# Second MLP: eight pairs plain on the first token pair instead of ten, the forming steps closer together

## The chip, the cores and the metric

The kernel runs on one core of one Trainium2 chip. The metric is the device time of one execution in microseconds (us). The kernel before took 2447.15 us, the median of three runs (2445.96, 2447.15, 2447.61).

Engines are named as in the profile: PE is the matmul engine (PEld its weight loads), DVE the vector engine, ACT the scalar engine, POOL the general engine, SP the engine whose queue issues the DMAs here.

## The reference

The reference is one step of a two-layer encoder over 1024 prompt tokens and 32 sample tokens, 1056 in all. What matters here is the second layer's MLP, the last large piece of work:

```python
u = x * (1 + sc2) + sh2
f = jnp.square(jax.nn.relu(u @ p['w_up'][l])) @ p['w_down'][l]
x = layer_norm(ALPHA * x + (1 + g2) * f, p['ln_g'][l, 1], p['ln_b'][l, 1])
```

D_MODEL is 1024 and D_FF is 4096. All data are float32.

## The kernel before

**Splits.** A float32 operand is held as two parts, high and low: ACT casts the high part (L89) and DVE subtracts it to get the low part (L90). Each product of a 128x128 block is then three matmuls (high by high, high by low, low by high), without the low by low.

**The second MLP** is `mlp7`, called once, with the settings of class `L1`. The 1056 tokens are four quarters of 264 (`QN`); two quarters are a token pair `tp`. Token pair 1 (quarters 3 and 2) comes first, token pair 0 second. The 4096 hidden columns are 16 pairs `pb` of 2x128 columns. For each hidden pair and token pair the up projection gives a 2x2 set of results, and it has two ways to do it:

- *Plain* (`up_tile`): for each of 2 column halves and 2 quarters, 24 matmuls of 264 columns (L118, L119, L120), 96 in all. It needs two split weight blocks of the pair (`w_up`, each loaded by a DMA of 512 KB into `raw_up` and split by one ACT and one DVE instruction of 128x1024).
- *Seven products* (class `Seven`, L1300): Winograd's form of the 2x2 product, with seven products of 12 matmuls, 84 in all. It needs formed weights (`forms`: sums and differences of the four weight blocks, four DVE subtractions of 128x512 and seven splits of 128x512, for each hidden pair once) and formed tokens (`tforms`, for each token pair once: in the sequence t3, ext, t1, TF, TF, u, 14 instructions of 128x1056 on DVE and 4 casts on ACT).

Either way four results are gathered in a tile `H`. When they are there, `h_forms` squares them, forms sums and differences for the down projection, splits them into `HL` and `HM` (one buffer each) and writes them to DRAM (`hd`, or `hpl` for pairs 14 and 15).

**The order.** Token pair 1 is ready before token pair 0, since the normalization (`norm`) that gives the tokens goes block by block. So a list `FIRST` of hidden pairs is done plainly on token pair 1 while the rest is made ready. Three of them come in the loop over `L.ready`; the others are `rest`. A counter `at` numbers the halves of `rest` so that the last has 13; a table says which forming steps are put in behind which half: step 0 is one step of `tforms` for token pair 1, step 1 one for token pair 0, step 2 one of `forms` for the first weights. After each pair of `rest`, the plain weights of the pair after next are asked for. Then the list `seq` gives the jobs of seven products: a pair in `FIRST` has the one job that is left (token pair 0), any other has two. Two jobs overlap on PE: the products are sorted by 7j+2i, for job j and product i. The variable `lone` is the last job on token pair 1; behind it the rooms of its tokens are given over to the loads `fx` of the down projection (`fill`, at products 2, 4, 6 from two jobs after `lone`), 14 tiles of 528 KB for its first group.

**What sets the order on the engines.** A scheduler places the instructions of DVE, ACT, SP and, in the plain part, PE by its own reckoning, from the order in the code; in the seven products PE's order is the code's (`manual_schedule`). Each engine then works through its own list strictly in order. The raw tiles of loaded weights, the tiles t3 and t1 of `tforms` and the loads `rdn_u` of `forms` share three buffers (`raw`); split weights share six (`wc`).

Of the kernel before, what the change touches and what calls it, by code (L numbers as in the profile page):

```python
# [75 lines left out]
def trunk_kernel(ctx: ExitStack, tc: tile.TileContext, a, o):  # L76
# [88 lines left out]
    def ada_part(l, i):  # L165
        return ada[:, l * 48 + i * KC:l * 48 + (i + 1) * KC, :]
# [954 lines left out]
    def up_weights(l, pb):  # L1121
        return [wblock(f"up{l}_{pb}_{i}", a["w_up"][l], 512 * i, pb * 256) for i in range(2)]

    def mlp7(L):
# [17 lines left out]
        def up_w(pb):  # L1142
            if pb not in wups:
                wups[pb] = up_weights(l, pb)
            return wups[pb]
# [33 lines left out]
        def up_tile(pb, f, q):  # L1179

            tp = q // 2
            ps = up_mm(pb, f, q)
            if (pb, tp) not in hts:
                hts[pb, tp] = [h_tile(pb, tp), 0]
            H = hts[pb, tp][0]
            nc.scalar.activation(H[:, ((1, 0), (3, 2))[f][q % 2]], ps, AF.Relu)
            hts[pb, tp][1] += 1
            if hts[pb, tp][1] == 4:
                h_forms(pb, tp, hts.pop((pb, tp))[0])
            flow.tick(QN / 96)  # L1190
# [9 lines left out]
        def tforms(tp, ext):  # L1200

            def b(i):
                kap, q = {B11: (0, 0), B12: (0, 1), B21: (1, 0), B22: (1, 1)}[i]
                return [L.u4(hl, tp, kap, q) for hl in range(2)]

            def raw(i):
                return raw_tile([P, 4, QN], f"t{i}_{l}_{tp}")

            def less(t, x, y):
                nc.vector.tensor_sub(t, x[0].bitcast(F32), y)  # L1210
                nc.vector.tensor_add(t, t, x[1].bitcast(F32))

            def diff(t, x, y):
                less(t, x, y[0].bitcast(F32))
                nc.vector.tensor_sub(t, t, y[1].bitcast(F32))
            t3 = raw(3)
            diff(t3, b(B22), b(B12))
            yield
            split(ext[:, 0], ext[:, 1], t3)
            yield  # L1220
            t1 = raw(1)
            diff(t1, b(B12), b(B11))
            yield
            split(TF[tp, 0][0], TF[tp, 0][1], t1)
            less(t1, b(B22), t1)
            yield
            split(TF[tp, 1][0], TF[tp, 1][1], t1)
            less(t1, b(B21), t1)
            yield
            split(*b(B12), t1)  # L1230
# [95 lines left out]
        seq = L.seq  # L1326
# [4 lines left out]
        def prep(n):  # L1331
            if n < len(makers):
                preps[n] = makers[n]()
                next(preps[n])
# [21 lines left out]
        for j, pb in enumerate(rest):  # L1356
            for f in range(2):
                for q in L.quarters[:2]:
                    up_tile(pb, f, q)
                if (j, f) == (0, 1):  # L1360
                    L.ready(2)
                    for n, tp in enumerate(L.pairs):
                        for i, t in enumerate(L.scratch(n)):
                            TF[tp, i] = t
                    exts[tp1] = ring.tile([P, 2, KG, QN], F32R, tag="wc", name=f"exu_{l}", bufs=6)
                    tfs = [tf, tforms(tp1, exts[tp1])]
                at = 2 * j + f - 2 * len(rest) + 14
                if at == 11:
                    prep(0)
                for n in {2: (1,), 3: (1,), 4: (1,), 5: (1,), 6: (1,), 7: (1,), 8: (0,), 9: (0,), 11: (0, 2),  # L1370
                          12: (2,), 13: (2, 0)}.get(at, ()):
                    if n < 2:
                        next(tfs[n], None)
                    else:
                        got[0] = next(preps[0])
            del wups[pb]
            if j + 2 < len(rest):
                up_w(rest[j + 2])
# [48 lines left out]
        with tc.manual_schedule(engines={mybir.EngineType.PE}):  # L1427
            for _, j, i in sorted((7 * j + 2 * i, j, i) for j in range(len(jobs)) for i in range(7)):
                n, tp = jobs[j]
# [439 lines left out]
    for ti in rev:  # L1869
        t0, n = TBS[ti]  # L1870
# [33 lines left out]
        for k in range(KC):  # L1904
            gain_shift(ti, 1, k)
    wup1 = {}
    FIRST = [6, 7, 8, 9, 10, 11, 12, 13, 14, 15]

    def early_up(ti, pr):

        if ti == rev[-1] and pr:
            wup1[FIRST[pr - 1]] = up_weights(1, FIRST[pr - 1])
    out_proj([(0,), (1, 2, 3)], rev, wo_get, o_mov, ada_part(1, 2), end_out1, "b", width=[384, 384, 320],
             after_pr=early_up)

    class L1:
# [2 lines left out]
        order, blocks = rev, [(0, 288), (288, 256), (544, 256), (800, 256)]  # L1919
        pairs, quarters = (1, 0), (3, 2, 1, 0)  # L1920
        first = FIRST
        seq = [(pb, (0,) if pb in FIRST else (1, 0)) for pb in (0, 6, 1, 7, 2, 8, 3, 9, 4, 10, 5, 11, 14, 12, 15, 13)]

        def u(hl, k, q):
            return u2[q // 2][:, hl, k, q % 2 * QN:(q % 2 + 1) * QN]
# [40 lines left out]
        def after(blk):  # L1966
            t0, n = blk
            tiles = [(t, min(P, t0 + n - t)) for t in range(t0, t0 + n, P)]
            flow.add(norm_out(tiles, L1.put_out, L1.next_y, L1.gb, blk == L1.blocks[-1]), TAIL[0])
    mlp7(L1)  # L1970
    flow.finish()
    psD_cm.__exit__(None, None, None)
# [36 lines left out]
```

## Time and profile before

| | |
|---|---|
| median of three runs | 2447.15 us |
| the profiled execution, its own time | 2451.64 us |
| its span, first to last instruction | 2449.7 us |
| mean granted clock of PE | 0.993 |
| busy share of the span: PE, DVE, ACT, POOL | 97%, 78%, 45%, 7% |
| DMA over the span | 137 GB/s |

The profiled execution is 4.49 us longer than the median of the runs; of that, 1.94 us lie outside its span. In the span, the plain part of the second MLP runs from about 1731 us, its seven products from 1854 to 2083 us, the down projection from there to the end. The busy share of PE counts pipelined matmuls as busy from start to end, so the share of a stretch says only whether it stood still at all; how long a matmul takes of PE's time is seen in the distance from one start to the next.

### The profile page before, as it was taken

How to read it: one execution, taken by the hardware profiler on the slowest of the kernel's cores; microseconds unless marked ns; L12 is line 12 of the kernel's file. 1: busy time of each engine (PE TensorE's matmuls, PEld its weight loads, DVE VectorE, ACT ScalarE, POOL GpSimd, SP SyncE). 2: the span in 40 equal slices, each digit the busy share in tenths (PEclk: the TensorE clock that was granted, in tenths of full speed). 3: DMA queues.
4: the chain of work that ended last, by engine and by line, in shares of the span. 5: the costliest groups of instructions: out<-in, count | busy, mean ns of one | idle time of the engine just before them, and what ended most of it. 6: DMA issues, size and time to landing. Idle time of an engine off the chain costs nothing.

```text
span 2449.7 us, 42910 instructions
## 1 busy us (share of the span) xinstructions
PE 2386.9 (97%) x16580; PEld 2294.7 (94%) x16580; DVE 1919.8 (78%) x4340; ACT 1090.7 (45%) x2264; POOL 167.3 (7%) x315
## 2 busy tenths in 40 slices
PE   7999999999999999999999999999999999899997
PEld 4999999999999999999999977789999999899997
DVE  4899998788678678687488666755998888887878
ACT  4554456283212212212157466763776777222212
POOL 0211100000000000000000224420000000000003
PEclk9999999999999999999999999999999999999999
DMA  7432223412233233233223230041486779966642
GB/s 287 137 102 88 89 80 109 157 35 87 89 101 121 87 104 113 82 116 107 89 77 101 64 73 2 10 117 42 159 275 233 255 256 335 376 234 230 228 156 72
DMA packets 251503, 335.15 MB, mean 137 GB/s; under 512 B 12824, under 2 KB 201644, under 8 KB 250276
## 3 DMA queue, kind: packets, MB, share of 16 engines
q1 hardware_dynamic: 251300, 332.42, 41.4%
q8 instruction: 130, 2.13, 0.4%
q14 instruction: 73, 0.60, 0.1%
HBM read 255.50 MB, written 79.24 MB: 137 GB/s over the span
## 4 chain that ended last, share of the span: by engine, by line
PE 76%; DVE 12%; DMA 4%; ACT 3%; issue 2%; POOL 0%; SPq 0%; ACTq 0%; DVEq 0%; POOLq 0%
PE dn L1409 11%; PE up L1300 6%; PE up L118 6%; PE up L120 6%; PE up L119 6%; PE dn L119 5%; PE dn L118 5%; PE dn L120 5%; PE pv L1749 3%; PE s L1692 2%; PE pt L1727 2%; PE o L118 1%; PE o L119 1%; PE o L120 1%; DMA hd<-HL 1%
## 5 line engine op out<-in xcount | busy, mean ns | idle before, releaser
L1409 PE MATMUL dn<-fx,wf_d 128*128 128x264 f32 x2016 | 254.2, 285 | 6.9 <-DVE ACX L986 3.3
L1409 PEld LDWEIGHTS dn<-fx,wf_d 128*128 128x128 f32 x2016 | 248.7, 188 | 9.3 <-issue 2.9
L119 PE MATMUL dn<-h,w_dn 128*128 128x384 f32 (+1 forms) x768 | 249.5, 325 | 0.0
L118 PE MATMUL up<-U,w_up 128*128 128x384 f32 (+1 forms) x768 | 249.2, 324 | 0.0
L119 PE MATMUL up<-U,w_up 128*128 128x384 f32 (+1 forms) x768 | 247.9, 323 | 0.0
L118 PE MATMUL dn<-h,w_dn 128*128 128x384 f32 (+1 forms) x768 | 247.8, 323 | 0.0
L120 PE MATMUL up<-U,w_up 128*128 128x384 f32 (+1 forms) x768 | 247.6, 322 | 0.0
L120 PE MATMUL dn<-h,w_dn 128*128 128x384 f32 (+1 forms) x768 | 247.3, 322 | 0.0
L986 DVE SCALAR_TENSOR_TENSOR ACX<-dn,ada,ACX 128x264 f32<-128x264 f32 (+5 forms) x400 | 160.1, 426 | 52.6 <-PE dn L1409 39.6
L238 DVE SCALAR_TENSOR_TENSOR aacc<-rada,cs,aacc 128x256 f32<-128x256 f32 x448 | 190.1, 476 | 0.0
L986 DVE SCALAR_TENSOR_TENSOR acc<-dn,ada,acc 128x384 f32<-128x384 f32 (+2 forms) x256 | 119.2, 485 | 47.0 <-PE dn L120 45.6
L1025 ACT ACTIVATE r<-up 128x384 f32<-128x384 f32 (+1 forms) x96 | 44.3, 463 | 243.3 <-PE up L120 236.9
L119 PEld LDWEIGHTS dn<-h,w_dn 128*128 128x128 f32 x768 | 144.5, 188 | 0.2 <-DVE h L1028 0.2
L120 PEld LDWEIGHTS dn<-h,w_dn 128*128 128x128 f32 x768 | 144.5, 188 | 0.0
L120 PEld LDWEIGHTS up<-U,w_up 128*128 128x128 f32 x768 | 144.3, 188 | 0.0
L118 PEld LDWEIGHTS up<-U,w_up 128*128 128x128 f32 x768 | 144.2, 188 | 0.1
L119 PEld LDWEIGHTS up<-U,w_up 128*128 128x128 f32 x768 | 144.2, 188 | 0.0
L118 PEld LDWEIGHTS dn<-h,w_dn 128*128 128x128 f32 x768 | 143.9, 187 | 0.2
L1300 PE MATMUL up<-u,wf_u 128*128 128x264 f32 x1056 | 139.6, 284 | 1.3 <-ACT wf_u L89 0.6
L1300 PEld LDWEIGHTS up<-u,wf_u 128*128 128x128 f32 x1056 | 132.6, 188 | 1.9 <-ACT wf_u L89 0.8
L1027 DVE TENSOR_TENSOR r<-r 128x384 f32<-128x384 f32 (+1 forms) x96 | 49.9, 522 | 103.3 <-ACT h L1026 102.9
L89 ACT CAST w_up<-raw_up 128x1024 fp32r<-128x1024 f32 x52 | 54.3, 1046 | 136.4 <-DMA raw_up<-in_w_up_dram 102.5
(386 smaller groups left out, 6575.0 us busy)
## 6 DMA issues: line engine op xcount, KB each, us to landing
rada<-in_w_ada_dram SPq DMA_DIRECT2D x64, 512.0 KB
hd<-HL SPq DMA_DIRECT2D x28, 1056.0 KB
raw_up<-in_w_up_dram SPq DMA_DIRECT2D x52, 512.0 KB
fx<-hd SPq DMA_DIRECT2D x50, 528.0 KB
hd<-HM SPq DMA_DIRECT2D x28, 792.0 KB
raw_dn<-in_w_down_dram SPq DMA_DIRECT2D x36, 512.0 KB
ada_room<-in_w_ada_dram SPq DMA_DIRECT2D x32, 512.0 KB
rdn_u<-in_w_up_dram SPq DMA_DIRECT2D x32, 512.0 KB
```

The source lines that it names most:

```text
L89: nc.scalar.copy(dst_h, src)
L118: nc.tensor.matmul(ps, wh, mov(0, k), start=(k == 0), stop=False)
L119: nc.tensor.matmul(ps, wh, mov(1, k), start=False, stop=False)
L120: nc.tensor.matmul(ps, wl, mov(0, k), start=False, stop=(k == nk - 1))
L238: nc.vector.scalar_tensor_tensor(acc[:, cnd], raw[:, k], sc, acc[:, cnd], op0=ALU.mult, op1=ALU.add)
L986: nc.vector.scalar_tensor_tensor(xs, ps[:, off + o:off + o + mm_], gate[:, fc, cnd:cnd + 1], xs, op0=ALU.mult, op1=ALU.add)
L1027: nc.vector.tensor_mul(r, r, r)
L1300: nc.tensor.matmul(p, self.ws[w][:, wl, k], moving(f, tp, xl, k), start=first and k + n_ == 0, stop=k == 3 and n_ == 2, skip_group_check=n ...
L1409: nc.tensor.matmul(p, ws[w][:, wl, k], t[:, s0, xl], start=first and k + n_ == 0, stop=k == kg - 1 and n_ == 2, skip_group_check=not first)
L1692: nc.tensor.matmul(s[:, b, :w], qst, kk[i][:, g, k0 + j0:k0 + j0 + w], start=(i == 0), stop=(i == 1))
L1727: nc.tensor.transpose(pt[:kp, j - j0, pr * P:(pr + 1) * P], ps_[pr][:, j * P:j * P + kp], ident)
L1749: nc.tensor.matmul(pv[64 * e:64 * e + 64, :nq], V[:kp, vt0 + j, g * 64:(g + 1) * 64], pts[e][:kp, j, :nq], start=(j == 0), stop=(j == nt - 1))
```

## The change

Two hidden pairs, 6 and 7, leave `FIRST`. On token pair 1 they are done by seven products instead of plainly, so there are 24 jobs of seven products instead of 22, and `rest` is five pairs instead of seven. The order of `seq` is made anew for that: three times two pairs with two jobs stand side by side, and the jobs behind `lone` are five instead of six. The counter `at` now runs from 4 to 13, and `tforms` for token pair 0 has its steps at 5, 6, 7, 8, 8, 9 instead of 2 to 7; the steps for token pair 1 are at 9, 10, 11, 13 instead of 8, 9, 11, 13. The steps for the first weights stay where they were, counted from the end.

```diff
-                for n in {2: (1,), 3: (1,), 4: (1,), 5: (1,), 6: (1,), 7: (1,), 8: (0,), 9: (0,), 11: (0, 2),
+                for n in {5: (1,), 6: (1,), 7: (1,), 8: (1, 1), 9: (1, 0), 10: (0,), 11: (0, 2),
                           12: (2,), 13: (2, 0)}.get(at, ()):
...
-    FIRST = [6, 7, 8, 9, 10, 11, 12, 13, 14, 15]
+    FIRST = [8, 9, 10, 11, 12, 13, 14, 15]
...
-        seq = [(pb, (0,) if pb in FIRST else (1, 0)) for pb in (0, 6, 1, 7, 2, 8, 3, 9, 4, 10, 5, 11, 14, 12, 15, 13)]
+        seq = [(pb, (0,) if pb in FIRST else (1, 0)) for pb in (0, 8, 1, 9, 2, 3, 10, 4, 5, 11, 6, 7, 14, 12, 15, 13)]
```

The first place is DVE's list from the point where the tokens of pair 0 are complete. `H1_9_1` is the tile of hidden pair 9 on token pair 1, `t3_1_0` and `t1_1_0` are the forming tiles of token pair 0, `w_up1_12_0` the first plain weight block of pair 12. Before:

```order
L1170 TENSOR_TENSOR H1_9_1_18851<-H1_9_1_18851 128x528
L1210 TENSOR_TENSOR t3_1_0_19046<-u2_0_18049 128x1056
L1211 TENSOR_TENSOR t3_1_0_19046<-t3_1_0_19046,u2_0_18049 128x1056
L90 TENSOR_TENSOR HL1_9_1_18961<-H1_9_1_18851,HL1_9_1_18961 128x4x264
L1215 TENSOR_TENSOR t3_1_0_19046<-t3_1_0_19046,u2_0_18049 128x1056
L1173 TENSOR_TENSOR H1_9_1_18851<-H1_9_1_18851 128x264
L1170 TENSOR_TENSOR H1_10_1_19018<-H1_10_1_19018 128x528
L1174 TENSOR_TENSOR H1_9_1_18851<-H1_9_1_18851 128x264
L90 TENSOR_TENSOR exu_1_18982<-t3_1_0_19046,exu_1_18982 128x1056
L90 TENSOR_TENSOR w_up1_12_0_19118<-raw_up1_12_0_19116,w_up1_12_0_19118 128x1024
```

And now:

```order
L1210 TENSOR_TENSOR t3_1_0_18983<-u2_0_18049 128x1056
L90 TENSOR_TENSOR HL1_11_1_18961<-H1_11_1_18851,HL1_11_1_18961 128x4x264
L1211 TENSOR_TENSOR t3_1_0_18983<-t3_1_0_18983,u2_0_18049 128x1056
L1173 TENSOR_TENSOR H1_11_1_18851<-H1_11_1_18851 128x264
L1215 TENSOR_TENSOR t3_1_0_18983<-t3_1_0_18983,u2_0_18049 128x1056
L1174 TENSOR_TENSOR H1_11_1_18851<-H1_11_1_18851 128x264
L90 TENSOR_TENSOR w_up1_13_0_18989<-raw_up1_13_0_18987,w_up1_13_0_18989 128x1024
L90 TENSOR_TENSOR HM1_11_1_18968<-H1_11_1_18851,HM1_11_1_18968 128x3x264
L1170 TENSOR_TENSOR H1_12_1_19022<-H1_12_1_19022 128x528
L1210 TENSOR_TENSOR t1_1_0_19116<-u2_0_18049 128x1056
```

At the same point of the norm, the first weights to be split behind it are those of the sixth pair of `FIRST` now (pair 13), and were those of the seventh (pair 12).

The second place is SP's list, from the DMA that writes the normalized tokens to DRAM (`xsp2`), at the same point of the norm. Before:

```order
L1865 DMA xsp2_79<-ACC0_17431 128x4x384
L96 DMA raw_up1_12_0_19116<-in_w_up_dram 128x4x256
L1865 DMA xsp2_79<-ACC1_17432 128x4x384
L1172 DMA hd1_3_1_18345<-HL1_9_1_18961 128x4x528
L96 DMA raw_up1_12_1_19121<-in_w_up_dram 128x4x256
```

And now:

```order
L1865 DMA xsp2_79<-ACC0_17431 128x4x384
L96 DMA raw_up1_13_0_18987<-in_w_up_dram 128x4x256
L1865 DMA xsp2_79<-ACC1_17432 128x4x384
L1172 DMA hd1_4_1_18347<-HL1_11_1_18961 128x4x528
L96 DMA raw_up1_13_1_18992<-in_w_up_dram 128x4x256
```

The loads of pair 13 stand where those of pair 12 stood: the writes of the tokens and of an `HL` are ahead of them.

The third place is DVE's list at the last plain weights, those of pair 15, and the first formed weights (`wf_u1_0_0`, of hidden pair 0). Before:

```order
L90 TENSOR_TENSOR w_up1_15_0_19521<-raw_up1_15_0_19519,w_up1_15_0_19521 128x1024
L90 TENSOR_TENSOR HL1_13_1_19504<-H1_13_1_19419,HL1_13_1_19504 128x4x264
L90 TENSOR_TENSOR TF0_18980<-t1_1_1_19447,TF0_18980 128x1056
L1173 TENSOR_TENSOR H1_13_1_19419<-H1_13_1_19419 128x264
L1210 TENSOR_TENSOR t1_1_1_19447<-u2_1_17466,t1_1_1_19447 128x1056
L1174 TENSOR_TENSOR H1_13_1_19419<-H1_13_1_19419 128x264
L1211 TENSOR_TENSOR t1_1_1_19447<-t1_1_1_19447,u2_1_17466 128x1056
L90 TENSOR_TENSOR HM1_13_1_19511<-H1_13_1_19419,HM1_13_1_19511 128x3x264
L90 TENSOR_TENSOR w_up1_15_1_19526<-raw_up1_15_1_19524,w_up1_15_1_19526 128x1024
L90 TENSOR_TENSOR TF0_18980<-t1_1_1_19447,TF0_18980 128x1056
L90 TENSOR_TENSOR wf_u1_0_0_19650<-rdn_u1_0_0_19642,wf_u1_0_0_19650 128x512
```

And now:

```order
L90 TENSOR_TENSOR u2_0_18049<-t1_1_0_19116,u2_0_18049 128x4x264
L90 TENSOR_TENSOR HM1_13_1_19251<-H1_13_1_19155,HM1_13_1_19251 128x3x264
L1211 TENSOR_TENSOR t1_1_1_19257<-t1_1_1_19257,u2_1_17466 128x1056
L1215 TENSOR_TENSOR t1_1_1_19257<-t1_1_1_19257,u2_1_17466 128x1056
L90 TENSOR_TENSOR w_up1_15_0_19263<-raw_up1_15_0_19261,w_up1_15_0_19263 128x1024
L90 TENSOR_TENSOR w_up1_15_1_19268<-raw_up1_15_1_19266,w_up1_15_1_19268 128x1024
L90 TENSOR_TENSOR TF0_18980<-t1_1_1_19257,TF0_18980 128x1056
L90 TENSOR_TENSOR HL1_14_1_19381<-H1_14_1_19296,HL1_14_1_19381 128x4x264
L1210 TENSOR_TENSOR t1_1_1_19257<-u2_1_17466,t1_1_1_19257 128x1056
L90 TENSOR_TENSOR wf_u1_0_0_19396<-rdn_u1_0_0_19388,wf_u1_0_0_19396 128x512
```

The weights of pair 15 stand ahead of both TF splits of token pair 1 now (one of the two stood ahead of the second block before), and all forming of token pair 0 stands ahead of them, as before.

## The prediction

> **What bounds the kernel now.** I read the page first, then what PE waited for in the plain part, then busy time by stretch, and then the order of time on DVE, SP and ACT from 1790 to 1876 us. The page's first rows:
>
> ```profile
> span 2449.7 us, 42910 instructions
> PE 2386.9 (97%) x16580; PEld 2294.7 (94%) x16580; DVE 1919.8 (78%) x4340; ACT 1090.7 (45%) x2264; POOL 167.3 (7%) x315
> ```
>
> PE bounds the kernel as a whole, but the change touches two short stages in which something else is as full. The stretches (the columns are length, then PE, PEld, DVE, ACT, POOL busy, granted clock, DMA share, GB/s):
>
> ```profile
> 1780.00:1800.00 20.00, 20.00 (x166) 20.00 (x166) 19.85 (x32) 17.07 (x28) 0.00 (x0) 1.00 0.74 257
> 1800.00:1820.00 20.00, 17.29 (x139) 16.87 (x139) 19.16 (x22) 13.38 (x19) 0.00 (x0) 1.00 0.94 311
> 1820.00:1840.00 20.00, 20.00 (x166) 19.95 (x165) 20.00 (x22) 13.86 (x20) 0.00 (x0) 1.00 0.78 261
> 1900.00:1950.00 50.00, 50.00 (x413) 50.00 (x412) 43.32 (x75) 36.62 (x63) 0.00 (x0) 1.00 0.69 240
> 2080.00:2100.00 20.00, 17.13 (x128) 15.69 (x127) 18.22 (x43) 8.26 (x15) 0.00 (x0) 1.00 1.02 359
> 2100.00:2120.00 20.00, 17.69 (x139) 16.93 (x139) 17.70 (x51) 5.39 (x14) 0.00 (x0) 1.00 1.02 386
> ```
>
> From 1780 to 1840 DVE is busy 59 of 60 us: the plain part has no DVE time left. In the seven products (1900 to 1950) PE never stands and DVE is 87% busy. At the start of the down projection (2080 on) the DMA engines are full and PE stands some 2.5 us in 20. What PE waited for from 1740 to 1860:
>
> ```profile
> PE up L118 <- ACT w_up L89: 2.0, 1, 2.0
> PE up L120 <- DVE w_up L90: 0.9, 2, 0.7
> ```
>
> So already now PE's only waits in the plain part are for split weights.
>
> **What the change saves on PE.** The rows: a product's 12 matmuls, and where the fourth plain pair starts.
>
> ```profile
> 1768.45 0.29 PE L118 MATMUL up<-u,w_up 128*128 128x264 f32 x1
> 1900.96 1.61 PE L1300 MATMUL up<-u,wf_u 128*128 128x264 f32 x12
> 1902.41 1.62 PE L1300 MATMUL up<-exu,wf_u 128*128 128x264 f32 x12
> 1854.18 2.01 PE L1300 MATMUL up<-u,wf_u 128*128 128x264 f32 x15
> ```
>
> Twelve matmuls take 1.46 us from start to start, 0.122 each. A plain pair is 96 x 0.122 = 11.7 us, a job of seven products 84 x 0.122 = 10.2. Two pairs moved save 24 matmuls, 2.9 us, if PE is the bound. The plain part loses 23.4 us of PE work, the seven products gain 20.5.
>
> **What it does to DVE in the plain part.** DVE's rows give the prices, from one start to the next:
>
> ```profile
> 1792.89 1.02 DVE L844 TENSOR_TENSOR u<-ut_n,u 128x384 fp32r<-128x384 f32 x2
> 1793.82 0.70 DVE L1170 TENSOR_TENSOR H<-H 128x528 f32<-128x528 f32 x1
> 1816.20 1.25 DVE L1210 TENSOR_TENSOR t<-u,t 128x1056 f32<-128x1056 f32 x1
> 1817.37 0.42 DVE L1173 TENSOR_TENSOR H<-H 128x264 f32<-128x264 f32 x1
> 1817.71 1.25 DVE L1211 TENSOR_TENSOR t<-t,u 128x1056 f32<-128x1056 f32 x1
> 1819.23 1.22 DVE L90 TENSOR_TENSOR w_up<-raw_up,w_up 128x1024 fp32r<-128x1024 f32 x1
> 1820.36 1.25 DVE L90 TENSOR_TENSOR TF<-t,TF 128x1056 fp32r<-128x1056 f32 x1
> 1821.53 0.97 DVE L90 TENSOR_TENSOR HM<-H,HM 128x792 fp32r<-128x792 f32 x1
> 1822.42 1.25 DVE L1210 TENSOR_TENSOR t<-u,t 128x1056 f32<-128x1056 f32 x1
> 1852.26 0.68 DVE L1265 TENSOR_TENSOR s_u<-s_u,rdn_u 128x512 f32<-128x512 f32 x1
> 1852.86 0.68 DVE L1266 TENSOR_TENSOR s_u<-rdn_u 128x512 f32<-128x512 f32 x1
> ```
>
> A row of 1056 columns costs 1.17, of 1024 1.14, of 792 0.89, of 528 0.62, of 264 0.34, of 512 0.60 us. A plain pair costs DVE two weight splits and its h_forms: 2 x 1.14 + 0.62 + 1.17 + 2 x 0.34 + 0.89 = 5.6 us. Two pairs fewer free 11.3 us of DVE while PE loses 23.4 us. The 28 instructions of tforms (33 us) all stay. DVE, full before, now sets the pace. POOL does nothing here; ACT has room (13 to 17 of 20).
>
> I follow DVE's new list from the point at which the tokens of pair 0 are complete. Before, the next instruction starts at 1793.8. Ahead of it the new list has two weight splits less and one subtraction of 528 more: 1792.2. From there to the splits that PE needs, instruction by instruction:
>
> - first block of pair 13: 4 x 1.17 + 2 x 0.34 + 1.14 = 6.5, so 1798.7
> - second block: 0.89 + 0.62 + 4 x 1.17 + 1.14 = 7.3, 1806.0
> - first of pair 14: 4 x 1.17 + 2 x 0.34 + 0.89 + 1.14 = 7.4, 1813.4
> - the split of u, which ends the forming of token pair 0: pair 14's second block 1.8, then 6 x 1.17 + 0.68
> - first of pair 15: 0.89 + 2 x 1.17 + 1.14 = 4.4 more; the second directly behind it
>
> The loads can make it later. How long they take, by a load of SP and the cast on ACT that waited for it:
>
> ```profile
> 1798.60 4.74 SPq L96 DMA_DIRECT2D raw_up<-in_w_up_dram  x2
> 1806.13 1.05 ACT L89 CAST w_up<-raw_up 128x1024 fp32r<-128x1024 f32 x1 [0.32 <-DMA raw_up<-in_w_up_dram]
> 1828.96 1.85 SPq L96 DMA_DIRECT2D raw_up<-in_w_up_dram  x2
> 1834.36 1.05 ACT L89 CAST w_up<-raw_up 128x1024 fp32r<-128x1024 f32 x1 [0.53 <-DMA raw_up<-in_w_up_dram]
> ```
>
> That is 5.4 to 7.5 us, and then 1.05 for the cast. Pair 14's first load needs the buffer of pair 13's second block (free at 1806.0), so its split ends between 1813.7 and 1815.8; I take 1814.4, the second block 1816.2, the split of u 1823.9, pair 15's first block 1828.2. Pair 15's second load needs the buffer of t1, free with the split of u: 1823.9 + 5.4 to 7.5 + 1.05 + 1.14 is 1831.5 to 1833.6; I take 1832, nearer the lower end, since fewer DMAs stand beside it. What the loads pass on SP (the token write and an HL ahead of pair 13's blocks) stands where it stood.
>
> PE: three pairs behind it at 1768.45, it has done two more by 1768.45 + 23.4 = 1791.8, and pair 13's weights come at 1798.7: it waits 6.9 us. After such a wait the clock drops:
>
> ```profile
> 1730.47 0.57 PE L864 MATMUL var_n<-qr_n,ones_d 128*128 128x384 f32 x1 [4.09 <-ACT qr_n L89]
> 1732.00:1734.00 2.00, 2.00 (x10) 2.00 (x10) 1.66 (x3) 1.65 (x3) 0.00 (x0) 0.50 0.67 198
> 1734.00:1736.00 2.00, 2.00 (x18) 2.00 (x18) 1.57 (x2) 1.13 (x3) 0.00 (x0) 0.99 0.72 232
> 1807.22 0.39 PE L118 MATMUL up<-u,w_up 128*128 128x264 f32 x1 [1.99 <-ACT w_up L89]
> ```
>
> For 3.5 us after a gap of 4.1 the clock was a half; after one of 2.0 it was not (1.00 in its stretch). So 16 matmuls take 3.5 us and 32 take 3.9: pair 13's first half ends at 1806.1, which hides the slow clock under the wait for the second block. Then 48 x 0.122 = 5.9, 1812.0; wait to 1814.4; 11.7, 1826.1; wait to 1828.2; 18 matmuls, 1830.4; wait to 1832; 78 matmuls, 9.5. The seven products start at 1841.5 instead of 1854.2: **-12.7 us**, not -23.4. [...]
>
> **Prices on DVE, weighed.** The duration column says 1.25 where starts are 1.17 apart. [...] Charged to the queue it would make my 36 instructions up to the weights of pair 15 about 2.9 us longer. The spacing decides: 1.17.
>
> **The seven products.** Two more jobs: 14 products x 1.46 = **+20.5 us**; PE did not wait here before, and DVE pays per job less than 10.2 us.
>
> Their start is later supplied. From 1832 DVE has 5.9 us to the first formed weights of pair 0 (4 x 1.17 + 2 x 0.60); the second raw block, loaded into the buffer freed at 1832, makes it 1839.2; then 6.5 (3 x 1.17 + 5 x 0.60) to the weights of the third product, 1845.7. PE wants them at 1841.5 + 2.9 = 1844.4: **+1.3 us**. DVE ends u of token pair 1 at 1849.8. Before:
>
> ```profile
> 1851.08 1.26 DVE L90 TENSOR_TENSOR u<-t,u 128x1056 fp32r<-128x1056 f32 x1
> 1858.24 0.69 DVE L1264 TENSOR_TENSOR s_u<-rdn_u,rdn_u 128x512 f32<-128x512 f32 x1 [1.08 <-DMA rdn_u<-in_w_up_dram]
> 1875.89 1.28 DVE L90 TENSOR_TENSOR wf_u<-rdn_u,wf_u 128x512 fp32r<-128x512 f32 x2
> ```
>
> From the end of u (1852.3) to the next pair's sums were 6.0 us (a load into the freed buffer), from there to the third pair's weights 17.7. Now: 1855.8 and 1873.5 plus 0.6. The nineteenth product wants them at 1841.5 + 1.3 + 18 x 1.46 = 1869.1; before it was 1880.5 against 1876.5. So PE waits 5.0 us, or less by DVE's own waits in the 17.7 us, which a DVE that is behind will not have. Bounds 0 and 5.0; I take **+3 us**.
>
> **The end of the seven products.** One single job fewer lies between the rooms becoming free and the end. It moved 1056 + 792 + 2 x 512 KB, 2.9 MB:
>
> ```profile
> hd<-HL SPq DMA_DIRECT2D x28, 1056.0 KB
> hd<-HM SPq DMA_DIRECT2D x28, 792.0 KB
> rdn_u<-in_w_up_dram SPq DMA_DIRECT2D x32, 512.0 KB
> ```
>
> At the 359 to 386 GB/s shown that is 8 us of full DMA, while PE's time for it is 10.2: **+1.9 us** of backlog, which PE then waits. Bounds: -2 (DVE also has a job less) and +4.
>
> Sum: -12.7 + 20.5 + 1.3 + 3 + 1.9 = +14.0. The profiled execution (2449.7 in span, 2451.6 in all) would go to 2465.6; on the median of 2447.15 it is **2461**.
>
> **Rivals.**
>
> - *DVE's queue alone* (no wait for loads): pair 15's blocks at 1827.2 and 1828.4, start at 1838.9, -15.3 + 20.5 and nothing after: +5.2, 2452.4. For it: ACT's two load waits shown are under 0.6 us. Against: two buffers are freed only by the forming itself.
> - *PE stays the bound*: -2.9, 2444.2, faster. It needs pair 13 split at 1791.8 and pair 15 by 1815.2, so the queue would have to be 6.9 and 13 us shorter. Only a DVE list worked off in another way could do it; 59 of 60 us speak against it.
> - *More waits*: loads at 7.5 us (+1.6), 5.0 instead of 3, +4 at the end: 2461.2 + 1.6 + 2 + 2.1 = 2467, and 3 more if the shorter waits drop the clock: 2470.
>
> **How the numbers follow.** A measurement here tells about 0.2%, 4.9 us, from no change. The likeliest case, 0.64, has 2455 to 2466. DVE's queue alone 0.17 (half of it within 0.2%), PE the bound 0.05, more waits 0.14. Leaving out PE's case and the ends of the outer two gives 2452 to 2468. Faster 0.05, same 0.09, slower 0.86.
>
> **What would show it.** Right: PE waits on w_up of some 13 us in the plain part, one of them about 7 us with a half clock after it; the first L1300 matmul at 1840 to 1844; DVE full to 1850; a wait of L1300 on wf_u in its first 30 us, where none was. Wrong: no wait over 3 us on w_up, the first L1300 before 1835, or PE standing still less at the start of the down projection than before.

## The result

| | before | after |
|---|---|---|
| median of the runs (6 each, beside each other) | 2447.24 us | 2461.81 us |
| lowest to highest | 2445.96 to 2447.95 | 2456.66 to 2466.77 |
| ratio, 95% interval | | 1.0053 (1.0043 to 1.0063) |
| profiled execution: span, granted clock | 2449.7 us, 0.993 | 2460.6 us, 0.991 |

The change makes the kernel 0.5% slower: 2461.81 us where 2461 was forecast. Between the two profiled executions the span grows by 10.9 us, between the medians the time by 14.6. A second set of runs of both gave 1.0052 (1.0038 to 1.0065). In the rows below, VectorE, ScalarE and GpSimd are DVE, ACT and POOL.

The waits of PE in the plain part and at the hand-over, of after (what PE waited for: us in total, times, longest):

```profile
PE up L118 <- ACT w_up L89: 3.7, 3, 2.7
PE up L120 <- DVE w_up L90: 2.9, 4, 1.1
PE up L1300 <- ACT H L1303: 2.5, 1, 2.5
```

That is 6.6 us on w_up, where the prediction had some 13, and a wait of 2.5 us at the seven products' start, for which it had 1.3 us and another cause. The rows of PE in time order show the places:

```profile
1794.58 0.39 PE L118 MATMUL up<-u,w_up 128*128 128x264 f32 x1 [2.65 <-ACT w_up L89]
1797.02 0.59 PE L120 MATMUL up<-u,w_up 128*128 128x264 f32 x1 [1.08 <-DVE w_up L90]
...
1837.68 3.06 PE L1300 MATMUL up<-u,wf_u 128*128 128x264 f32 x24
1843.21 4.71 PE L1300 MATMUL up<-TF,wf_u 128*128 128x264 f32 x24 [2.48 <-ACT H L1303]
1847.77 1.61 PE L1300 MATMUL up<-u,wf_u 128*128 128x264 f32 x12
```

The seven products begin at 1837.68 (before: 1854.2). Two products later PE waits 2.48 us, and the 24 matmuls behind it take 4.71 us, where the first 24 took 3.06. Their clock, in the table of stretches (busy time by engine, then PEclk, the granted clock, and the DMA share):

```profile
1798.00:1802.00 4.00, 4.00 (x20) 4.00 (x19) 3.96 (x4) 2.50 (x3) 0.00 (x0) 0.50 0.99 352
1842.00:1846.00 4.00, 2.79 (x13) 2.79 (x14) 4.00 (x6) 1.68 (x4) 0.00 (x0) 0.67 0.40 135
```

So each of the two longer waits is followed by a stretch at half clock (0.50 from 1795.54 to 1802.37 and from 1843.33 to 1846.74). What PE waited for at 1843 is on ScalarE:

```profile
1839.81 1.07 ACT L89 CAST HL<-H 128x1056 fp32r<-128x1056 f32 x1
1840.79 0.61 ACT L89 CAST wf_u<-s_u 128x512 fp32r<-128x512 f32 x1
1841.30 1.07 ACT L89 CAST u<-t 128x1056 fp32r<-128x1056 f32 x1
1842.27 0.61 ACT L89 CAST wf_u<-rdn_u 128x512 fp32r<-128x512 f32 x1
1842.79 0.37 ACT L1303 COPY H<-up 128x264 f32<-128x264 f32 x1
```

Product 2 adds onto the PSUM bank of product 0, so it needs product 0 copied out first (L1303); that copy stood in ScalarE's queue behind casts that belong to the plain part and to the forming.

**Where the span went.** The program ahead of the second MLP is the same, yet profiled executions differ there by some us. So times are counted from one mark R ahead of everything that the change touches, the matmul behind a 4.1 us wait: for before it is the row at 1730.47 that the prediction shows, and for after:

```profile
1730.19 0.44 PE L864 MATMUL var_n<-qr_n,ones_d 128*128 128x384 f32 x1 [4.09 <-ACT qr_n L89]
```

S is the first matmul of the seven products, X the first that uses ext (the sixth product in PE's order), D the first of the down projection. S of before is the row at 1854.18 that the prediction shows, S of after the row at 1837.68 above. For X the first start in the rows by shape counts, of before:

```profile
L1300 PE MATMUL up<-ext,wf_u x72: 278/284/289, 1861.5 to 2016.2; 128*128 128x264 f32 x72
```

and of after:

```profile
L1300 PE MATMUL up<-ext,wf_u x96: 279/284/288, 1849.2 to 2034.6; 128*128 128x264 f32 x96
```

For D the rows of PE around the first matmul of the down projection (L1409), of before:

```profile
2080.10 0.53 PE L1409 MATMUL dn<-fx_e,wf_d 128*128 128x264 f32 x3
2080.47 1.62 PE L1300 MATMUL up<-u,wf_u 128*128 128x264 f32 x12
```

and of after:

```profile
2091.30 1.62 PE L1409 MATMUL dn<-fx_e,wf_d 128*128 128x264 f32 x12
```

| stretch | before | after | change | predicted |
|---|---|---|---|---|
| R to S (plain part) | 123.7 | 107.5 | -16.2 | -12.7 |
| S to X (five products; hand-over) | 7.3 | 11.5 | +4.2 | +1.3 |
| X to D (rest of the seven products) | 218.6 | 242.1 | +23.5 | +20.5 + 3 + 1.9 |
| D to the end | 369.6 | 369.3 | -0.3 | 0 |
| sum | 719.2 | 730.4 | +11.2 | +14.0 |

Two jobs more are 14 products of 1.45 us (1847.77 to 1849.2 above), 20.3; so X to D carries +3.2 of its own. Of that, 1.5 are a shift of the mark: before, three matmuls of the down projection stand ahead of the last product (2080.47), after, all stand behind it. With D put behind the last product in both, X to D grows by 22.0 and D to the end by 1.2, so 1.7 and 1.2 us are left beyond the two jobs. The plain part gained more than forecast, and the hand-over took most of the surplus back.

### The profile page after: what moved, and what is told of

It is laid out like the page before. It is cut to its first block, busy times and chain, and to the rows that moved or that the text cites. A ratio compares the mean times of both kernels' runs of the same rounds, so it can differ in the third digit from the quotient of the medians.

```text
span 2460.6 us, 42862 instructions
## 1 busy us (share of the span) xinstructions
PE 2388.4 (97%) x16556; PEld 2294.2 (93%) x16556; DVE 1918.9 (78%) x4342; ACT 1087.6 (44%) x2262; POOL 167.2 (7%) x315
## 4 chain that ended last, share of the span: by engine, by line
PE 77%; DVE 11%; ACT 3%; DMA 3%; issue 2%; POOL 0%; SPq 0%; DVEq 0%; ACTq 0%; POOLq 0%
PE dn L1409 11%; PE up L1300 7%; PE up L118 5%; PE up L120 5%; PE up L119 5%; PE dn L119 5%; PE dn L118 5%; PE dn L120 5%; PE pv L1749 3%; PE s L1692 2%; PE pt L1727 2%; PE o L118 1%; PE o L119 1%; PE o L120 1%; PE op_b L118 1%
## 5 line engine op out<-in xcount | busy, mean ns | idle before, releaser
L1409 PE MATMUL dn<-fx,wf_d 128*128 128x264 f32 x2016 | 254.4, 285 | 8.6 <-DVE ACX L986 5.1
L1409 PEld LDWEIGHTS dn<-fx,wf_d 128*128 128x128 f32 x2016 | 248.7, 188 | 11.0 <-DVE ACX L986 3.9
L1300 PE MATMUL up<-u,wf_u 128*128 128x264 f32 x1152 | 151.7, 284 | 1.0 <-ACT H L1303 1.0
L1300 PEld LDWEIGHTS up<-u,wf_u 128*128 128x128 f32 x1152 | 144.4, 188 | 1.4 <-ACT H L1303 1.2
```

The lines of the kernel that those rows point to most:

```text
L1300: nc.tensor.matmul(p, self.ws[w][:, wl, k], moving(f, tp, xl, k), start=first and k + n_ == 0, stop=k == 3 and n_ == 2, skip_group_check=n ...
L1409: nc.tensor.matmul(p, ws[w][:, wl, k], t[:, s0, xl], start=first and k + n_ == 0, stop=k == kg - 1 and n_ == 2, skip_group_check=not first)
```

## The experiments

In all of them the kernel before ran beside; ratios are to it. The times from R of the profiled executions, in us:

| kernel | jobs | S | X | D | end | median | ratio, 95% interval |
|---|---|---|---|---|---|---|---|
| before | 22 | 123.7 | 131.0 | 349.6 | 719.2 | | |
| ten, closer table | 22 | 120.4 | 129.6 | 348.4 | 718.1 | 2448.74 | 0.9997 (0.9986 to 1.0007) |
| ten, closer, exchanged | 22 | 120.2 | 130.3 | 350.2 | 720.6 | 2451.30 | 1.0007 (0.9998 to 1.0015) |
| ten, GpSimd | 22 | 138.8 | 149.0 | 369.3 | 739.1 | 2469.69 | 1.0077 (1.0062 to 1.0092) |
| nine, closer table | 23 | 117.4 | 130.8 | 360.7 | 732.0 | 2460.88 | 1.0044 (1.0028 to 1.0061) |
| after | 24 | 107.5 | 119.0 | 361.1 | 730.4 | 2461.81 | 1.0053 (1.0043 to 1.0063) |
| after again | 24 | 107.2 | 118.6 | 359.9 | 729.0 | 2462.98 | 1.0052 (1.0038 to 1.0065) |
| after, GpSimd | 24 | 126.4 | 135.3 | 376.2 | 747.5 | 2477.40 | 1.0108 (1.0093 to 1.0123) |
| after, less VectorE work | 24 | 103.7 | 111.4 | 352.1 | 723.3 | 2454.91 | 1.0026 (1.0015 to 1.0037) |
| after, exchanged | 24 | 107.5 | 116.1 | 359.5 | 730.5 | 2460.89 | 1.0050 (1.0037 to 1.0063) |
| after, gaps filled | 24 | 107.5 | 117.5 | 362.8 | 733.4 | 2462.96 | 1.0061 (1.0048 to 1.0073) |
| after, own places | 24 | 110.2 | 117.9 | 359.1 | 728.9 | 2459.50 | 1.0041 (1.0028 to 1.0053) |
| after, other tail | 24 | 109.0 | 119.0 | 360.2 | 729.2 | 2461.98 | 1.0046 (1.0033 to 1.0060) |
| after, own places, late forming | 24 | 102.7 | 118.4 | 358.8 | 730.3 | 2461.26 | 1.0046 (1.0031 to 1.0060) |

### The closer table alone, on ten pairs

```
 FIRST = [6, 7, 8, 9, 10, 11, 12, 13, 14, 15]        (as before)
-for n in {2: (1,), 3: (1,), 4: (1,), 5: (1,), 6: (1,), 7: (1,), 8: (0,), 9: (0,), 11: (0, 2),
+for n in {5: (1,), 6: (1,), 7: (1,), 8: (1, 1), 9: (1, 0), 10: (0,), 11: (0, 2),
```

> Ten pairs plain as before, with the closer table of forming steps alone. Theory (VectorE's in-order list sets the start of the seven products, and what counts is how much work is in it): the list holds the same work in another order, so within 3 us of before, 2446 to 2450. Rival (the closer steps are what costs): most of the 14.6 us, 2457 to 2462, with waits on w_up in the plain part as long as with eight pairs (6.6 us).

No difference: 0.9997. Behind R and up to 1860 us PE has one wait, for the same copy as above:

```profile
PE up L1300 <- ACT H L1303: 1.6, 1, 1.6
```

There is no wait on w_up left, so with ten pairs the closer table does no harm: it even takes the 2.9 us of before away, and 1.6 come back at the hand-over. What costs in the change is the number of pairs, with the order of jobs that goes with it.

### Nine pairs plain

```
-FIRST = [8, 9, 10, 11, 12, 13, 14, 15]
+FIRST = [7, 8, 9, 10, 11, 12, 13, 14, 15]
-seq ... (0, 8, 1, 9, 2, 3, 10, 4, 5, 11, 6, 7, 14, 12, 15, 13)
+seq ... (0, 7, 1, 8, 2, 9, 3, 10, 4, 5, 11, 6, 14, 12, 15, 13)
```

> Nine pairs plain, the closer table, 23 jobs. Theory: TensorE loses 11.7 us of plain work, VectorE 5.7 us; the seven products start 6 to 8 us earlier than before's 1854.2 (by the profile), one more job costs 10.2: 2450 to 2454. Rival (the loss is the clock's, which drops only after waits as long as with eight pairs): start 11 us earlier and 2446 to 2448.

S came 6.3 us earlier, as the theory had it, but the time missed its range: 2460.9. PE's waits:

```profile
PE up L120 <- DVE w_up L90: 3.4, 2, 2.7
PE up L1300 <- ACT H L1303: 3.0, 1, 3.0
PE up L118 <- ACT w_up L89: 2.0, 1, 2.0
```

The stretches behind the 3.0 us wait, in the columns as above:

```profile
1852.00:1856.00 4.00, 1.60 (x7) 1.60 (x8) 4.00 (x6) 2.87 (x6) 0.00 (x0) 0.72 0.61 187
1856.00:1860.00 4.00, 4.00 (x20) 4.00 (x20) 3.67 (x7) 0.90 (x2) 0.00 (x0) 0.50 1.03 331
```

At the hand-over PE waits 3.0 us and then runs at half clock, and X is where it was before (130.8 against 131.0): the earlier start is gone five products later, and the job more is paid in full. The expectation had priced the start and the job more, and nothing at the hand-over. The copy is again late in ScalarE's queue: ScalarE works almost without a gap from 1848.55, where a result of the plain part (PE) releases it, to the copy at 1853.99.

### Low parts of the weights on GpSimd

```
-def up_weights(l, pb):
-    return [wblock(f"up{l}_{pb}_{i}", a["w_up"][l], 512 * i, pb * 256) for i in range(2)]
+def up_weights(l, pb, eng=None):
+    return [wblock(f"up{l}_{pb}_{i}", a["w_up"][l], 512 * i, pb * 256, eng) for i in range(2)]
...
-wups[pb] = up_weights(l, pb)
+wups[pb] = up_weights(l, pb, nc.gpsimd)
```

On eight pairs:

> After, with the low parts of the weights of pairs 11 to 15 (ten blocks of 1.14 us) formed by GpSimd, idle there, instead of VectorE. Theory (VectorE's list is the bound of the plain part): the list is 11.4 us shorter, TensorE's waits of 6.6 us on w_up nearly vanish and the clock stays up, the seven products start at 1829 to 1832 instead of 1837.7, and the time falls by 5 to 9 us to 2453 to 2457, with less spread. Rival (the loads into the raw buffers are the bound): start at 1836 to 1838, 2459 to 2462. Rival (GpSimd's subtraction is so slow, or slows VectorE so much, that the weights come later): start after 1839, 2463 or more.

On ten:

> Before, with the low parts of the weights of pairs 9 to 15 formed by GpSimd. Theory: the 2.9 us that TensorE stands still for w_up go, 2443 to 2446. Rival (loads): no change, 2447. Rival (GpSimd too slow): slower, 2449 or more.

Both went the way of the third case: a ratio of 1.0108 where after has 1.0053, and of 1.0077 where before has 1. A row of GpSimd, with eight pairs:

```profile
1828.52 2.44 POOL L90 TENSOR_TENSOR w_up<-raw_up,w_up 128x1024 fp32r<-128x1024 f32 x1 [6.34 <-ACT w_up L89]
```

and VectorE at the same time:

```profile
1827.47 1.25 DVE L1215 TENSOR_TENSOR t<-t,u 128x1056 f32<-128x1056 f32 x1
1828.64 3.45 DVE L1211 TENSOR_TENSOR t<-t,u 128x1056 f32<-128x1056 f32 x1
```

VectorE's second instruction ends at 1832.1, 1.1 us after GpSimd's. Between 1764 and 1840 us VectorE begins five instructions of 128x1056 beside a row of GpSimd, this one among them; they take 2.56 to 3.49 us and end 1.11 to 1.13 after it. Alone such an instruction takes 1.17 from start to start, so these five look as if they did their work once GpSimd was done. The split that was moved to GpSimd did not leave VectorE free; it held it for 2.2 us, where it would itself have taken VectorE 1.14. For the question of VectorE against the loads the two runs therefore decide nothing.

### After again

> The changed kernel unchanged, beside the three that follow, so that they have their reference in the same runs. All theories: a ratio to before of 1.004 to 1.006 and times that spread over some 10 us.

1.0052, times from 2457.38 to 2464.21. From R it stands within 1.4 us of the first profile at every mark.

### Less work for VectorE

```
 def less(t, x, y):
     nc.vector.tensor_sub(t, x[0].bitcast(F32), y)
-    nc.vector.tensor_add(t, t, x[1].bitcast(F32))

 def diff(t, x, y):
     less(t, x, y[0].bitcast(F32))
-    nc.vector.tensor_sub(t, t, y[1].bitcast(F32))
```

> After, with 12 of the 28 VectorE subtractions and additions that form the products' sums of u left out (the low parts of u are left out of these sums, so the output is less exact): 14 us less in VectorE's list before the seven products, the loads and everything else kept. Theory (VectorE's list is the bound of the plain part): the waits of 6.6 us on w_up shrink under 2 us, the seven products start at 1829 to 1833 instead of 1837.7, and the time is 5 to 9 us under after's. Rival (the loads of weights into the raw buffers are the bound): start at 1836 or later, within 2 us of after.

The time fell by 8 us (2454.91 against 2462.98 beside it), as the theory had it; S by only 3.5 to 3.8, and X by 7.2 to 7.6, because the wait on product 0's copy is gone as well. PE's waits:

```profile
PE up L118 <- ACT w_up L89: 4.2, 3, 3.3
```

The waits on VectorE's split are gone, those on ScalarE's cast have stayed: 4.2 us, where the theory had under 2. The longest, 3.3 us, is ScalarE's own queue. Ahead of the cast stand the last result of the pair before, for which ScalarE waited, its square and another cast (between the rows shown):

```profile
1791.09 0.39 ACT L1186 ACTIVATE H<-up 128x264 f32<-128x264 f32 x1 [0.97 <-PE up L120]
...
1793.24 1.04 ACT L89 CAST w_up<-raw_up 128x1024 fp32r<-128x1024 f32 x1
```

In the two short ones (0.2 and 0.7 us) the cast waits for the load, as in the second of them:

```profile
1808.18 1.05 ACT L89 CAST w_up<-raw_up 128x1024 fp32r<-128x1024 f32 x1 [1.64 <-DMA raw_up<-in_w_up_dram]
```

So VectorE binds from the plain part to the first jobs, and ScalarE's queue and the loads lie close behind it. In after, too, the 2.65 us at 1794 end with a cast that ScalarE reaches only after working without a gap from 1783.3; VectorE's split, the 1.08 us behind it, comes last there. VectorE's 14 us account for 8 of the 14.6 us that the change costs: at 1.0026 the kernel is still slower than before. What the same 12 instructions would be worth on ten pairs was not tried.

### Products 2 and 3 of the first job exchanged

```
-sevens[j].product(i, up_end if j == len(jobs) - 1 else None)
+sevens[j].product({2: 3, 3: 2}.get(i, i) if j == 0 else i, up_end if j == len(jobs) - 1 else None)
```

> After, with products 2 and 3 of the first of the 24 jobs exchanged, so that TensorE has 1.46 us of work on another PSUM bank while ScalarE's queue comes to the copy of product 0. Theory: the wait of 2.5 us at 1843 falls to about 1.0, which is too short to drop the clock, so 1.5 of wait and 1.7 to 2.2 of half clock go: 3 to 4 us under after. Rival (the weights' casts on ScalarE or VectorE stand right behind the copy and end the same wait): 0 to 1 us.

The wait fell to 0.42 us, now on formed weights, and 0.33 us on the copy:

```profile
1841.32 1.48 PE L1300 MATMUL up<-TF,wf_u 128*128 128x264 f32 x10 [0.42 <-DVE wf_u L90]
1843.13 1.73 PE L1300 MATMUL up<-TF,wf_u 128*128 128x264 f32 x12 [0.33 <-ACT H L1303]
```

X came 2.5 to 2.9 us earlier. Of that, 0.4 to 1.6 is left at D, and nothing at the end, since in this execution PE ran at half clock for a stretch of the down projection (granted clock 0.50 from 2102.6 to 2109.4). The median is 2.1 us under that of after, with intervals that overlap: between the two expectations, and undecided. The place and the releaser of the wait are shown; its worth in the end is not.

### The gaps filled with matmuls

```
+if j == 1:
+    fill_pe(24, up_w(pb)[0][:, 0, 0, 0:P], L.u(0, 0, L.quarters[0]))
...
+if j == 0 and i == 2:
+    fill_pe(16, got[n][1][:, 0, 0], moving(B21, tp, 0, 0))
```

(fill_pe issues so many matmuls into a PSUM tile that nobody reads.)

> After, with 24 matmuls whose result nobody reads put into the wait ahead of pair 13 (2.9 of its 3.7 us) and 16 into the wait ahead of the first job's product 2 (1.95 of its 2.5 us). Theory (waits of 2.5 us and more halve the clock, and this is why after's times spread): no half clock at 1795 to 1802 and at 1843 to 1848, the time 2 to 4 us under after's and its spread at most half of after's 10 us. Rival (the spread and the loss come from elsewhere): median and spread like after's.

The clock behaved as expected; at both places it stays whole:

```profile
1798.00:1802.00 4.00, 4.00 (x36) 4.00 (x35) 3.97 (x5) 2.93 (x3) 0.00 (x0) 1.00 0.91 332
1842.00:1846.00 4.00, 3.49 (x29) 3.28 (x28) 4.00 (x7) 1.69 (x4) 0.00 (x0) 1.00 0.68 228
```

The time did not (2462.96 against 2462.98). S is at 107.5 with and without the half clock at 1795, so that one was hidden under the wait for pair 13's second block. The other did cost: X is 1.1 to 1.5 earlier. But D is 1.7 to 2.9 later than after's, without one large wait: PE's short waits from X to D sum to 3.6 us instead of 1.9, and why X to D took 245.3 us instead of 241.3 to 242.1 stays open beyond that. A half clock also remained in the down projection (0.50 from 2105.5 to 2112.3), where nothing was filled. The times spread over 4.0 us, in after over 6.8 and 10.1; with five and six runs that is a hint.

### Own places for the working tiles

```
-t3 = raw(3)
+t3 = ext[:, 1]
...
-t1 = raw(1)
+t1 = TF[tp0, 1][0] if tp == tp1 else raw(1)
```

> After, with t3 of token pair 1 and of token pair 0 formed in the place of its own low part and t1 of token pair 1 in a place of TF that is still free, so that only t1 of token pair 0 takes one of the three raw buffers, which the loads of weights then have (these sums are rounded once more, so the output is less exact; the instructions are the same in number and kind). Theory (with VectorE's list 14 us shorter the seven products still began only some 3.5 us earlier, because the load for pair 13 was issued where a raw buffer came free: the buffers bind beside VectorE): the loads of pairs 13 and 15 are issued earlier, the waits on w_up fall from 6.6 to 2 to 4 us, the start moves 2 to 4 us earlier, the time 2 to 5 us under after's. Rival (VectorE's list alone): the loads land earlier and their splits still wait for their turn in the list: start and time within 1.5 us of after.

The loads came earlier, and PE waited all the same: for pair 15 the cast is done at 1818.6, and the split waits for its turn in VectorE's list. The cast on ScalarE (lines stand one to three higher in this kernel):

```profile
1817.57 1.05 ACT L90 CAST w_up<-raw_up 128x1024 fp32r<-128x1024 f32 x1 [1.26 <-DMA raw_up<-in_w_up_dram]
```

The splits of both blocks on VectorE:

```profile
1825.28 2.35 DVE L91 TENSOR_TENSOR w_up<-raw_up,w_up 128x1024 fp32r<-128x1024 f32 x2
```

PE's row for the wait:

```profile
1826.55 0.59 PE L121 MATMUL up<-u,w_up 128*128 128x264 f32 x1 [4.36 <-DVE w_up L91]
```

And the clock behind it:

```profile
1826.00:1830.00 4.00, 3.45 (x15) 3.46 (x16) 4.00 (x5) 0.46 (x1) 0.00 (x0) 0.50 0.57 168
```

The wait, in one piece, halved the clock where nothing hid it, and S came 2.7 us later, not earlier. That is the rival's mechanism, with a clock cost that neither expectation had. X came 0.7 to 1.1 earlier, the time is 1.0041.

### Products exchanged, on ten pairs with the closer table

The same edit as above, on the ten pairs with the closer table.

> Ten pairs plain with the closer table, and products 2 and 3 of the first job exchanged. The ten pairs with the closer table alone waited 1.6 us for the copy of product 0 and no longer on w_up. Theory: that wait goes, 1 to 2 us under the ten pairs with the closer table, so a ratio to before of 0.998 to 0.9995: the fastest of the kernels here, if only just. Rival (the formed weights end the same wait): a ratio of 0.9995 to 1.0005.

1.0007: no gain. The wait for a copy of L1303 moved to a later product and was 2.2 us there:

```profile
1858.73 3.01 PE L1300 MATMUL up<-ext,wf_u 128*128 128x264 f32 x12 [2.24 <-ACT H L1303]
```

Neither expectation had that. No kernel here is faster than before by more than its interval.

### Another tail of the jobs

```
-seq ... (0, 8, 1, 9, 2, 3, 10, 4, 5, 11, 6, 7, 14, 12, 15, 13)
+seq ... (0, 8, 1, 9, 2, 3, 4, 10, 5, 6, 7, 11, 14, 12, 15, 13)
```

> After, with the jobs in another order: the last job of token pair 1 three places earlier (0, 8, 1, 9, 2, 3, 4, 10, 5, 6, 7, 11, 14, 12, 15, 13), so that one more single job lies behind the point where the rooms for the down projection's loads come free, as before. Theory (the prediction's +1.9 us: the loads are one job late): the waits of the down projection's first matmuls fall by about 2 us and the time is 1 to 3 us under after's. Rival (the loads move what the queue can, all the way to the end, and come no earlier): within 1 us of after.

The waits at the end of the seven products and the start of the down projection that bear on this, of after from 2070 to 2150 us:

```profile
PE dn L1409 <- DVE ACX L986: 5.1, 5, 1.9
PE dn L1409 <- DMA fx<-hd: 0.6, 2, 0.3
```

and of this kernel from 2075 to 2150 us:

```profile
PE dn L1409 <- DVE ACX L986: 2.6, 3, 1.0
PE up L1300 <- ACT wf_u L89: 1.5, 1, 1.5
PE dn L1409 <- DMA fx<-hd: 0.9, 1, 0.9
```

ACX holds the sums to which VectorE adds each result of the down projection; PE waits there until VectorE has read a result out of PSUM. These waits fall from 5.1 us (4.0 in after's second execution) to 2.6, so they do hang on the order of the jobs. That the loads `fx` are behind it isn't shown: PE waits 0.6 us for them in after and 0.9 here. And a wait of 1.5 us on formed weights, with a half clock behind it (the longest matmul on `u` in the seven products takes 554 ns here, 391 in after), takes their place, and the end is where it was (729.2 against 729.0 and 730.4). The medians (ratio 1.0046 against 1.0052 and 1.0053) can't tell 1 us from 2.

### The same work for VectorE in another order

On the kernel with its own places:

```
-for n in {5: (1,), 6: (1,), 7: (1,), 8: (1, 1), 9: (1, 0), 10: (0,), 11: (0, 2),
-          12: (2,), 13: (2, 0)}.get(at, ()):
+for n in {5: (1,), 6: (1,), 7: (1,), 10: (1,), 11: (1, 2),
+          12: (1, 0, 2), 13: (0, 0, 2, 0)}.get(at, ()):
```

> The kernel whose working tiles stand in places of their own (t3 and one t1 out of the raw buffers, one rounding more), with the last three forming steps of token pair 0 and all remaining ones of token pair 1 moved behind the splits of pair 15's weights: the same work in VectorE's list, in another order. There pair 15's splits had stood in the list 8 us behind their casts, TensorE had waited 4.4 us for them, and the clock halved. Theory (what binds from the plain part to the seven products' first jobs is the amount of VectorE work, so a wait that is removed at one place comes back at the next): the seven products start 6 to 8 us earlier, at 1832 to 1834, the waits of the first two jobs on formed weights and sums grow by about as much, and the time is within 3 us of the kernel with its own places, 2457 to 2462. Rival (the order is at fault, not the amount): no new waits, 5 to 9 us faster, 2451 to 2455.

As the theory had it. S is 7.5 us earlier than with own places alone (102.7), the earliest of all, and then, in PE's rows:

```profile
1836.10 0.59 PE L1303 MATMUL up<-TF,wf_u 128*128 128x264 f32 x1 [4.81 <-ACT TF L90]
1837.39 5.18 PE L1303 MATMUL up<-TF,wf_u 128*128 128x264 f32 x23 [0.71 <-DVE TF L91]
```

PE waits 5.5 us for sums that are now formed later, and runs at half clock after it (granted clock 0.50 from 1838 to 1842). X is 118.4 and the end 730.3, as after's. With the same VectorE work, S ranges over 7.5 us (102.7 to 110.2) and X over 2.9 (116.1 to 119.0); only with 12 instructions fewer is X at 111.4. So X hangs first on the amount of VectorE's work ahead of the seven products' first jobs; the order moves the wait from one place to another, and X by no more than 2.9. The amount alone doesn't explain nine pairs: with 5.6 us less on VectorE than ten pairs with the same table, X is no earlier there (130.8 against 129.6), and it was ScalarE's copy and a half clock that took the start back.

## Why the prediction was right or wrong

**The sum was right, partly by terms that offset each other.** 2461.81 against 2461, inside the range, on the side that was given 0.86. That the two lie within 1 us is luck: between the profiles the time grew by 11.2 us, where the terms add up to 14.0. Term by term, from R:

- *Plain part, -12.7*: measured -16.2. The list on VectorE was full as foreseen, and PE stood before pair 13 at the foreseen time (1794.58 less 2.65 is 1791.9; forecast 1791.8). But all splits came about 2 us earlier than worked out, since the list itself began earlier: VectorE is through with the tokens of pair 0 at 1790.4 instead of 1792.2. The forecast went from before's 1793.8, and so took over the 2.1 us that VectorE had stood still for ScalarE behind R; in after that is 0.95 us. The last block of pair 15 came at 1828.3 instead of 1832. That last step failed: the load into the buffer of t1 was put on the path at 5.4 to 7.5 us, and from its issue to the cast it took 4.1. It held VectorE up by no more than 0.73 us:

```profile
1821.92 0.37 SPq L96 DMA_DIRECT2D raw_up<-in_w_up_dram  x1
1826.03 1.05 ACT L89 CAST w_up<-raw_up 128x1024 fp32r<-128x1024 f32 x1 [0.39 <-DMA raw_up<-in_w_up_dram]
1827.11 1.23 DVE L90 TENSOR_TENSOR w_up<-raw_up,w_up 128x1024 fp32r<-128x1024 f32 x1 [0.73 <-ACT w_up L89]
```

  The rival of VectorE's queue alone had the start at 1838.9; 1837.68 is close to that. In the run with own places the loads came earlier, and the start did not.
- *The half clock behind the first wait, hidden*: right; S is the same without it.
- *Waits before pairs 14 and 15 at full clock, and 3 us in the third rival if not*: an estimate between the two gaps of before, 2.0 us at full clock and 4.1 with half clock behind it; no run shows the 3 us. In after PE waited 0.21 and 0.66 us there for pair 14 and 0.86, 0.89 and 0.23 for pair 15, and the clock was 1.00 from 1802.4 to 1843.3.
- *Two more jobs, +20.5*: right, 20.3.
- *Third product, +1.3, on VectorE's weights*: the place was right, the size and the releaser were wrong. It waited 2.48 us for the copy of product 0 in ScalarE's queue, and half clock followed; S to X grew by 4.2. The prediction looked at VectorE's queue here and not at ScalarE's. Where the exchange takes this wait away, the formed weights stand 0.42 us behind it, so the predicted wait was real and covered.
- *Nineteenth product, +3*: no such wait came in after. PE reached that product at 1868.2, near the forecast 1869.1, but VectorE was ahead of its forecast: u of token pair 1 ended at 1845.3 instead of 1849.8, and the next pair's sums began at 1851.6 instead of 1855.8, after a wait for their own load:

```profile
1851.60 0.69 DVE L1264 TENSOR_TENSOR s_u<-rdn_u,rdn_u 128x512 f32<-128x512 f32 x1 [4.68 <-DMA rdn_u<-in_w_up_dram]
```

  It isn't the delay at 1843 that gave VectorE this time: with the products exchanged X is 2.5 to 2.9 us earlier, and the wait doesn't come either. The bounds of 0 and 5.0 held, the value taken in them did not.
- *End of the seven products, +1.9*: the size is near (1.7 us up to the last product, 1.2 behind it), the mechanism isn't shown. The loads were to be late, but PE waits 0.6 us for `fx` (before: 0.8) and 5.1 us for VectorE's adds to ACX (before: 3.3). Nor does the working give 1.9: 2.9 MB at 359 to 386 GB/s against 10.2 us leave 2.1 to 2.7. The other tail shows that the waits at the down projection's start follow the order of the jobs, and not that an order brings the time back.

**The main reason held**: PE's 23.4 us less were never to be had, since VectorE kept most of its list. The run with less VectorE work shows it, and the late forming shows that another order doesn't bring the time back. What the prediction lacked is that this bound does not end with the plain part. It put the waits on w_up where they are largest and the hand-over at 1.3; in fact a start won early is lost again by the sixth product, with eight pairs 4.2 of 16.2 us and with nine all of it, and the queue at which PE stands there is ScalarE's.

**What would show it wrong**: one of the signs against it came, no single wait on w_up over 3 us: the longest is 2.65. Of those for it, PE's waits on w_up were half of the 13 us, the first L1300 matmul stood 2 us ahead of its range of 1840 to 1844, VectorE was full to 1847 instead of 1850, and the wait of L1300 was for a copy and not for wf_u. The first three erred on the same side, VectorE being earlier than worked out.

The profiles account for 11.2 of the 14.6 us between the medians. The mean clock of after's six runs was 0.988 to 0.994, and the longer ones had the lower clock (2456.66 us: 0.994; 2466.77: 0.989). By an estimate from these, 0.005 of 2460 us is 12 us of full clock, as much as the 10.1 us between the two. So more stretches at half clock can well be the rest; the last section shows where they come and go.

## What to carry to other kernels

Work taken from the busiest engine comes back as time only as far as the engine that feeds it is relieved too (here 23.4 us less for PE made the plain part 16.2 us shorter); count that engine's whole list up to the point where the next phase runs by itself, since reordering it or ending one wait moves the wait on. At a hand-over between two phases look at every queue that the new phase's first small operations join, ScalarE's too: in after one copy behind four casts cost 2.5 us and a stretch at half clock. And price a new wait of 2 to 5 us with the clock that it may cost, unless another wait hides it: here one of 2.48 us and one of 4.36 each had 3.4 us or more at half clock behind it.

## What the hardware showed unexpectedly

- Waits of PE shorter than foreseen bring half clock: one of 2.48 us, and one of 2.65 followed by 1.08. Waits of 0.86, 0.89 and 0.23 us from 1824 to 1828 in after did not. Two waits of one size can go either way: with nine pairs, 1.97 and 0.75 us brought it,

```profile
1806.00:1809.41 3.41, 1.11 (x6) 0.89 (x7) 2.31 (x4) 2.92 (x4) 0.00 (x0) 1.00 0.71 267
1809.41:1812.82 3.41, 3.41 (x18) 3.41 (x17) 3.41 (x5) 1.99 (x4) 0.00 (x0) 0.50 0.97 294
```

  and in before 1.99 and 0.73 us did not:

```profile
1805.73:1809.14 3.41, 1.84 (x13) 1.63 (x13) 3.31 (x4) 3.05 (x5) 0.00 (x0) 1.00 1.04 388
1809.14:1812.56 3.42, 2.77 (x22) 2.77 (x23) 3.42 (x5) 2.46 (x4) 0.00 (x0) 1.00 1.00 319
```

  These stretches are not chosen freely. In all 14 traces the granted clock changes only at points of a grid of 3.413 us, and where the grid lies differs between executions. A stretch of this grid at full clock in which PE was busy for less than 1.54 us was followed by one at half clock every time, one with more than 2.03 us never, of 9840 such stretches. So by these counts it matters how much of a wait falls into one stretch. The prediction let waits of 2.4 and 2.1 us pass at full clock; in after, one of 2.48 us was enough for the half. The grid also fits the wider spread of the kernels with several waits of that size: of the nine kernels with 24 jobs, seven have a half clock of 3.4 or 6.8 us at the start of the down projection, the second execution of after among them (granted clock 0.57 from 2100 to 2104), and the first has none (1.00 there). No run shifted the grid against the same program.
- Beside a subtraction of 128x1024 on GpSimd (2.4 to 3.8 us) five of VectorE's instructions of 128x1056 took 2.56 to 3.49 us instead of 1.25.
- The same program ahead of R reaches it between 1725.5 and 1731.9 us in the profiled executions. That is half of what this change moves, so profiles of a change this small are compared from a common mark.
